# Fewer, larger tiles in four buffers, with split first loads and split last stores, in a blockwise max-pool-and-subtract kernel

## The chip, the cores and the metric

The kernel runs on one core of a Trainium2 chip. The metric is the device time of one execution in microseconds (us). The kernel before took 628.7 us, the median of four runs that lie between 628.33 and 629.75 us. A profile of one execution goes with it: the busy time of each engine, the traffic of the core's 16 DMA engines, and each instruction with its start, its duration and what it waited for.

## The reference

```python
B, C, H, W = 8, 64, 256, 256          # x: float32
x_r = x.reshape(B, C, 32, 8, 32, 8)
pooled = x_r.max(axis=(3, 5))         # max of every 8x8 block
upsampled = np.repeat(np.repeat(pooled, 8, axis=2), 8, axis=3)
return (x - upsampled).astype(np.float32)
```

Every 8x8 block of every image has its own maximum subtracted. The input and the output are 134.22 MB each.

## The kernel before, in words

The input is seen as 16,384 rows of 2,048 floats (8 KB). One such row is eight lines of an image, so it holds 32 whole blocks. A **strip** is 128 of these rows, one in each partition of on-chip memory: 1 MB. There are 128 strips in all. A tile of R strips holds, in each partition, R rows that follow one another in main memory, so that one partition's share of a transfer is one contiguous run of R x 8 KB.

The list `TILES` (L11) gives 32 tiles of four strips each. The first is loaded in two pieces of two strips, the next 30 are whole, the last is loaded in pieces of two, one and one. In this kernel a piece is the unit for loading, computing and storing alike. `BUFS = 6` (L12) gives six buffers of 32 KB per partition for the tiles, 192 KB together.

For each tile the loop at L64 takes a buffer, issues all its loads on the queue of SyncE (SP, L77), and then, piece by piece, calls `pool_and_subtract` (L36) and issues the store on the queue of ScalarE (ACT, L80). All arithmetic is on VectorE (DVE): one max-reduction for the piece (L48 for more than one strip, L41 for one strip) and then one in-place subtraction for each strip (L55). The subtraction's result overwrites the loaded data, and the store goes out of the same buffer.

The order is that of the program on each engine (L62 fixes it). Semaphores order the engines among themselves: a reduction waits for its load to land, a store waits for the last subtraction of its piece, and a load into a buffer that was used before waits until the store out of that buffer has landed. SP does nothing but issue loads, so a waiting load holds up later loads only; ACT does nothing but issue stores, so a waiting store holds up later stores only. The DMAs of both queues share the same few completion semaphores by turns, and an issue also waits until the DMA that used its semaphore earlier has landed.

Of the kernel before, what the change touches and what calls it, by code (L numbers as in the profile page):

```python
# [1 line left out]

# [4 lines left out]

F32 = mybir.dt.float32
ROW = 2048

TILES = [[2, 2]] + [[4]] * 30 + [[2, 1, 1]]  # L11
BUFS = 6  # L12


@with_exitstack
def kernel(
    ctx: ExitStack,
    tc: tile.TileContext,
    x: bass.AP,
    out: bass.AP,  # L20
):
    nc = tc.nc
    P = nc.NUM_PARTITIONS
    B, C, H, W = x.shape
    pH = pW = 8
    oW = W // pW

    x_rows = x.rearrange("b c (oh ph) w -> (b c oh) (ph w)", ph=pH)
    out_rows = out.rearrange("b c (oh ph) w -> (b c oh) (ph w)", ph=pH)
    assert sum(map(sum, TILES)) * P == x_rows.shape[0]  # L30
    size = max(map(sum, TILES))

    data = ctx.enter_context(tc.tile_pool(name="data", bufs=BUFS))
    small = ctx.enter_context(tc.tile_pool(name="small", bufs=BUFS))

    def pool_and_subtract(dat, tops, R):  # L36

        wins = dat.rearrange("p (r ph ow pw) -> p r ph ow pw", r=R, ph=pH, ow=oW)
        tops = tops.rearrange("p (r ow) -> p r ow", r=R)
        if R == 1:  # L40
            nc.vector.tensor_reduce(  # L41
                out=tops[:, 0],
                in_=wins[:, 0].rearrange("p ph ow pw -> p ow ph pw"),
                axis=mybir.AxisListType.XY,
                op=mybir.AluOpType.max,
            )
        else:
            nc.vector.tensor_reduce(  # L48
                out=tops,
                in_=wins.rearrange("p r ph ow pw -> p r ow ph pw"),  # L50
                axis=mybir.AxisListType.XY,
                op=mybir.AluOpType.max,
            )
        for r in range(R):
            nc.vector.tensor_tensor(  # L55
                out=wins[:, r],
                in0=wins[:, r],
                in1=tops[:, r].unsqueeze(1).unsqueeze(3).to_broadcast([P, pH, oW, pW]),
                op=mybir.AluOpType.subtract,
            )  # L60

    ctx.enter_context(tc.manual_schedule())  # L62
    at = 0
    for pieces in TILES:  # L64
        dat = data.tile([P, size * ROW], F32, name="dat")
        pooled = small.tile([P, size * oW], F32, name="pooled")
        parts = []
        done = 0
        for R in pieces:
            src = x_rows[at : at + P * R].rearrange("(p r) d -> p (r d)", r=R)  # L70
            dst = out_rows[at : at + P * R].rearrange("(p r) d -> p (r d)", r=R)
            part = dat[:, done * ROW : (done + R) * ROW]
            tops = pooled[:, done * oW : (done + R) * oW]
            parts.append((part, tops, dst, R))
            at += P * R
            done += R
            nc.sync.dma_start(out=part, in_=src)  # L77
        for part, tops, dst, R in parts:
            pool_and_subtract(part, tops, R)
            nc.scalar.dma_start(out=dst, in_=part)  # L80


# [1 line left out]
_INS = ['x']  # L84
_OUTS = [((8, 64, 256, 256), 'float32')]


# [23 lines left out]
```

## Time and profile before

| what | value |
|---|---|
| median of the runs | 628.7 us (628.33 to 629.75) |
| the profiled execution's own time | 628.33 us |
| its span, first to last instruction | 626.1 us |
| VectorE busy | 562.4 us, 90% |
| bytes moved | 268.46 MB, mean 429 GB/s |
| load of 4 strips, issue to landing (median) | 61.0 us |
| store of 4 strips, issue to landing (median) | 37.3 us |
| packets of 8, 16 and 32 KB, time of one on its DMA engine (packet records of the trace) | 309, 611 and 1213 ns |
| first load issued, first packet starts | 0.73 us, 1.72 us |
| last store issued, its last packet's end | 616.57 us, 624.81 us |

The span is shorter than the device time by 2.2 us, which lie before the first and after the last instruction. "GB/s" counts loads and stores together. The DMA share is the busy time of the 16 DMA engines over the stretch; it can come out a few per cent over 1.00, because records of packets overlap slightly and a packet is counted where it starts. A DMA of 128 partitions is cut into 128 packets, one for each partition, eight on each of the 16 engines; each packet is one contiguous run. A DMA's landing is the last of the 16 small writes to its semaphore, one from each engine.

### The profile page before, as it was taken

What the parts mean: (1) busy time and instruction counts of PE and PEld (TensorE: products, weight loads), DVE (VectorE), ACT (ScalarE), POOL (GpSimd) and SP (SyncE); (2) the same over time, 40 slices, a digit from 0 to 9 for tenths busy, and PEclk for the clock granted to TensorE, in tenths of its full rate; (3) what the DMA queues carried; (4) which work ended last, traced back from release to release, by engine and by line L of the source; (5) the groups of instructions that cost most, each with busy time, mean ns of one, the idle gap of its engine ahead of it and who ended that gap; (6) DMA issues with size and microseconds to landing.
All of it is one profiled execution on the core that took longest, in us unless ns stands there. A gap on an engine that the chain in (4) does not pass through costs nothing.

```text
span 626.1 us, 367 instructions
## 1 busy us (share of the span) xinstructions
DVE 562.4 (90%) x163; POOL 0.2 (0%) x4
## 2 busy tenths in 40 slices
DVE  4999999998898888988889988899888898899962
POOL 0000000000000000000000000000000000000000
DMA  9999999999999999999999999999999999999997
GB/s 366 426 421 436 425 435 435 435 435 433 435 433 434 435 435 433 431 429 431 425 435 435 435 433 433 435 433 435 435 435 433 435 427 427 431 431 432 430 442 340
DMA packets 10083, 268.46 MB, mean 429 GB/s; under 512 B 1120, under 2 KB 1120, under 8 KB 1120
## 3 DMA queue, kind: packets, MB, share of 16 engines
q1 hardware_dynamic: 5040, 134.22, 49.9%
q10 hardware_dynamic: 5040, 134.22, 49.7%
q14 instruction: 3, 0.02, 0.0%
HBM read 134.22 MB, written 134.22 MB: 429 GB/s over the span
## 4 chain that ended last, share of the span: by engine, by line
DVE 89%; another core or an unknown queue 7%; DMA 1%; issue 1%
DVE dat L55 45%; DVE pooled L48 44%; DMA dat<-in_x_dram 1%; DVE pooled L41 1%
## 5 line engine op out<-in xcount | busy, mean ns | idle before, releaser
L48 DVE TENSOR_REDUCE pooled<-dat 128x128 f32<-128x8192 f32 (+1 forms) x33 | 273.8, 8296 | 46.4 <-DMA dat<-in_x_dram 46.4
L55 DVE TENSOR_TENSOR dat<-dat,pooled 128x2048 f32<-128x2048 f32 x128 | 285.0, 2287 | 1.2
L41 DVE TENSOR_REDUCE pooled<-dat 128x32 f32<-128x2048 f32 x2 | 4.6, 2284 | 6.5 <-DMA dat<-in_x_dram 6.5
L95 POOL MEMSET const-bfloat16-1.0<- 128x1 bf16 x1 | 0.1, 101 | 0.0
L95 POOL MEMSET const-uint8-127<- 128x1 uint8 x1 | 0.1, 101 | 0.0
L95 POOL MEMSET const-float32-0.0<- 128x1 f32 x1 | 0.1, 98 | 0.2 <-issue 0.2
L95 POOL MEMSET const-float32-1.0<- 128x1 f32 x1 | 0.1, 98 | 0.0
## 6 DMA issues: line engine op xcount, KB each, us to landing
dat<-in_x_dram SPq DMA_DIRECT2D x30, 4096.0 KB, 61.0
out_dram<-dat ACTq DMA_DIRECT2D x30, 4096.0 KB, 37.3
dat<-in_x_dram SPq DMA_DIRECT2D x3, 2048.0 KB, 12.5
out_dram<-dat ACTq DMA_DIRECT2D x3, 2048.0 KB, 19.6
dat<-in_x_dram SPq DMA_DIRECT2D x2, 1024.0 KB, 66.3
out_dram<-dat ACTq DMA_DIRECT2D x2, 1024.0 KB, 13.0
```

Of the source, the lines that this page charges most:

```text
L41: nc.vector.tensor_reduce(out=tops[:, 0], in_=wins[:, 0].rearrange("p ph ow pw -> p ow ph pw"), axis=mybir.AxisListType.XY, op=mybir.AluOp ...
L48: nc.vector.tensor_reduce(out=tops, in_=wins.rearrange("p r ph ow pw -> p r ow ph pw"), axis=mybir.AxisListType.XY, op=mybir.AluOpType.max,)
L55: nc.vector.tensor_tensor(out=wins[:, r], in0=wins[:, r], in1=tops[:, r].unsqueeze(1).unsqueeze(3).to_broadcast([P, pH, oW, pW]), op=mybir ...
L95: nc = _bacc.Bacc("TRN2", target_bir_lowering=False, num_devices=1)
```

## The change

Loads and stores get lists of their own. A tile is now given by the pieces in which it is loaded and the pieces in which it is computed and stored.

- There are 22 tiles: one of four strips (loaded and stored as 1, 1, 2), one of six (3, 3 and 3, 3), 18 of six that are loaded and stored whole, one of six that is loaded whole and stored as 3, 3, and a last one of four that is loaded whole and stored as 2, 1, 1.
- There are four buffers of 48 KB per partition (192 KB as before).
- A piece is now a slice of columns of its tile. A partition's rows of the whole tile follow one another in main memory, so a piece of R strips is a run of R x 8 KB, and the runs of neighbouring partitions lie one whole tile row apart.

```diff
-TILES = [[2, 2]] + [[4]] * 30 + [[2, 1, 1]]
-BUFS = 6
+TILES = [([1, 1, 2], [1, 1, 2]), ([3, 3], [3, 3])] + [([6], [6])] * 18 + [
+    ([6], [3, 3]),
+    ([4], [2, 1, 1]),
+]
+BUFS = 4
...
-    for pieces in TILES:
+    for loads, stores in TILES:
         dat = data.tile([P, size * ROW], F32, name="dat")
         pooled = small.tile([P, size * oW], F32, name="pooled")
-        parts = []
-        done = 0
-        for R in pieces:
-            src = x_rows[at : at + P * R].rearrange("(p r) d -> p (r d)", r=R)
-            dst = out_rows[at : at + P * R].rearrange("(p r) d -> p (r d)", r=R)
-            part = dat[:, done * ROW : (done + R) * ROW]
-            tops = pooled[:, done * oW : (done + R) * oW]
-            parts.append((part, tops, dst, R))
-            at += P * R
-            done += R
-            nc.sync.dma_start(out=part, in_=src)
-        for part, tops, dst, R in parts:
-            pool_and_subtract(part, tops, R)
-            nc.scalar.dma_start(out=dst, in_=part)
+
+        rows = sum(loads)
+        src = x_rows[at : at + P * rows].rearrange("(p r) d -> p (r d)", r=rows)
+        dst = out_rows[at : at + P * rows].rearrange("(p r) d -> p (r d)", r=rows)
+        at += P * rows
+        lo = 0
+        for R in loads:
+            part = slice(lo * ROW, (lo + R) * ROW)
+            nc.sync.dma_start(out=dat[:, part], in_=src[:, part])
+            lo += R
+        lo = 0
+        for R in stores:
+            part = slice(lo * ROW, (lo + R) * ROW)
+            pool_and_subtract(dat[:, part], pooled[:, lo * oW : (lo + R) * oW], R)
+            nc.scalar.dma_start(out=dst[:, part], in_=dat[:, part])
+            lo += R
```

`pool_and_subtract` is not changed.

More of the change, by code (lines that the diff above doesn't have):

```diff
@@ L29 @@
     out_rows = out.rearrange("b c (oh ph) w -> (b c oh) (ph w)", ph=pH)
-    assert sum(map(sum, TILES)) * P == x_rows.shape[0]
-    size = max(map(sum, TILES))
+    assert sum(sum(loads) for loads, _ in TILES) * P == x_rows.shape[0]
+    size = max(sum(loads) for loads, _ in TILES)
     data = ctx.enter_context(tc.tile_pool(name="data", bufs=BUFS))
```

## The prediction

> **What bounds the kernel now.** I read the page first: the engines' busy time, the slices of DMA and GB/s, the queues.
>
> ```profile
> span 626.1 us, 367 instructions
> ...
> DVE 562.4 (90%) x163; POOL 0.2 (0%) x4
> ...
> DMA  9999999999999999999999999999999999999997
> GB/s 366 426 421 436 425 435 435 435 435 433 435 433 434 435 435 433 431 429 431 425 435 435 435 433 433 435 433 435 435 435 433 435 427 427 431 431 432 430 442 340
> ...
> q1 hardware_dynamic: 5040, 134.22, 49.9%
> q10 hardware_dynamic: 5040, 134.22, 49.7%
> ```
>
> Loads (q1) and stores (q10) together fill 99.6% of the 16 DMA engines' span. VectorE is 90% busy, but the chain of waits names it for the wrong reason: it lists what VectorE did while it stood waiting on loads in turn. The waits of VectorE and of SP's queue say so:
>
> ```profile
> DVE pooled L48 <- DMA dat<-in_x_dram: 46.4, 23, 8.8
> ...
> SPq L77 <- DMA out_dram<-dat: 501.2, 27, 19.3
> ```
>
> VectorE waits for loads, loads wait for stores to free buffers, and both run on engines that are never idle. So only three things can move the end: how long the bytes take, the idle time before the first packets, and the idle time at the end. Next the stretches (columns: stretch, length, VectorE busy, POOL busy, clock, DMA share, GB/s):
>
> ```profile
> 0.00:2.00 2.00, 0.00 (x0) 0.20 (x4) 1.00 0.65 123
> 2.00:4.00 2.00, 0.00 (x0) 0.00 (x0) 1.00 0.56 180
> 140.00:520.00 380.00, 344.45 (x100) 0.00 (x0) 1.00 1.00 433
> ...
> 612.00:616.50 4.50, 4.46 (x2) 0.00 (x0) 1.00 1.00 430
> 616.50:620.00 3.50, 0.03 (x1) 0.00 (x0) 1.00 0.96 410
> 620.00:623.00 3.00, 0.00 (x0) 0.00 (x0) 1.00 1.03 434
> 623.00:626.10 3.10, 0.00 (x0) 0.00 (x0) 1.00 0.10 40
> ```
>
> The reader should see a plateau of 433 GB/s from start to 623 us. At the head about 1.8 us are idle (first packet at 1.72 us). At the tail traffic stops at 623 to 624.8 us. The plateau is the span, so the rows for VectorE matter only as cover:
>
> ```profile
> L55 DVE TENSOR_TENSOR dat<-dat,pooled 128x2048 f32<-128x2048 f32 x128 | 285.0, 2287 | 1.2
> L48 DVE TENSOR_REDUCE pooled<-dat 128x128 f32<-128x8192 f32 x30 | 260.5, 8684 | 37.7 <-DMA dat<-in_x_dram 37.7
> L48 DVE TENSOR_REDUCE pooled<-dat 128x64 f32<-128x4096 f32 x3 | 13.2, 4415 | 8.8 <-DMA dat<-in_x_dram 8.8
> L41 DVE TENSOR_REDUCE pooled<-dat 128x32 f32<-128x2048 f32 x2 | 4.6, 2284 | 6.5 <-DMA dat<-in_x_dram 6.5
> ```
>
> **Step 1, packets.** The bytes stay; the packets get fewer. By the packet records 8, 16 and 32 KB take 309, 611 and 1213 ns: 301.3 ns per 8 KB and 7.7 ns per packet. The 433 GB/s plateau gives 16 x 32,768 B / 433 GB/s = 1210.8 ns between 32 KB packets, so about 5.5 ns each show in the wall time. Packets per engine before: 240 + 24 + 16 = 280 in each queue, 560. After, loads: 152 of 48 KB, 8 of 32, 16 of 24, 8 of 16, 16 of 8 = 200; stores: 144 of 48, 32 of 24, 16 of 16, 32 of 8 = 224; together 424. The 136 fewer save 0.75 us (5.5 ns) to 1.05 us (7.7 ns). DMAs fall from 70 to 53, 17 semaphore writes of 9 ns: 0.15 us. I take **-0.9 us**. A 48 KB packet isn't in the trace. At the low end it is one packet of 1815 ns; at the high end it is cut into three of 16 KB, then there are 1,016 packets, 456 more than before: +2.5 to +3.5 us; cut into 8 KB, 1,904 packets, +7.4 us or more. Each of the three sizes seen moved as one packet per partition, so I take one packet, and keep the cut as a rival.
>
> A rule that speaks against the ramp: the Trainium skill, "DMA: Bandwidth & Descriptors", section "Bandwidth", gives a 1 MB transfer 341 GB/s, 6.15 us, and advises larger ones. The change has six 1 MB transfers, before has four; by that figure two more cost an estimated 2 x (6.15 - 2.4) = 7.5 us. The stretch 620 to 623, all 1 MB stores, moved at 434 GB/s, so with the queue behind them they cost nothing here; the measurement decides.
>
> **Step 2, head.** The first load is 1 MB instead of 2, so its landing falls from 8.7 to about 6.3 us (2.4 us less data) and VectorE starts that much earlier. That is worth **0**: the DMA engines are the bound, and they run loads from 1.8 us either way. Four buffers hold 22 strips of loads, before 24; 22 x 2.42 us reach to 55 us with loads alone. The first buffer is free long before: VectorE ends tile 0 at 6.3 + 2 x 4.6 + 8.9 = 24.4 us, its stores land below 40 us. Seven load issues of 0.46 us each on SP lie beside 2.4 us or more of data each. Bounds -0.5 to +0.5 us.
>
> **Step 3, the middle.** A six-strip tile needs 2 x 8 x 1.813 = 29.0 us of DMA. VectorE needs 8.68 + 2 x 2.135 = 12.95 us for the reduction (2.135 is the step per strip between the rows for two and four strips) and 6 x 2.225 = 13.35 us for subtractions (8.90 us for four on the timeline), 26.4 us with the gaps. Cover is 2.6 us per tile, before 19.4 - 17.6 = 1.8. If it went, each of 19 tiles would cost its shortfall. A buffer's round is 4 x 29.0 = 116 us; less VectorE's 26.4, 89.6 us remain for a load and a store in flight. Each needs 29.0 us beside the other plus about 3.5 us (a store at 17.74 us had its first packet at 21.14), 65 together. So both queues have work and the engines don't idle: **0**. A store that waits for a semaphore that a load used last does no harm: before, VectorE ended a tile at 537.7 and its store left at 556.99, and the plateau held because loads took the share.
>
> **Step 4, the tail.** This is where something new can be late: the last tile is loaded whole, so nothing of it can start before all has landed. Count from t = 0, where tile 19 of 0 to 21 has landed in steady state. The load of tile 20 began 1.8 us earlier. It lands at 29.0. VectorE ends 19 at 26.4, waits to 29.0, then two pieces of three strips (6.55 + 6.7 = 13.25 each): stores issued at 42.3 and 55.5. The load of tile 21 (32 KB packets, 9.7 us alone) runs beside 48 KB stores. In the trace packets of the queues alternate one for one: the 16 KB load beside 32 KB stores took 14.7 us (570.9 to 585.6) for 4.9 us of work, a third. So this load gets 1213 / (1213 + 1815) = 40% and takes 24.2 us: 27 + 24.2 = 51.3, landed about 53.3. VectorE is busy to 55.5, so the whole load is hidden, by 2.2 us. Then 8.9 us for two strips and 4.6 us for each of the last: stores issued at 64.4, 69.0, 73.6.
>
> The DMA work left at t = 0: load 20 13.6, load 21 9.7, stores 18 and 19 14.0 + 14.5 (18 was issued at -2.6), store 20 14.6, store 21 9.8, together 76.2 us, plus whatever backlog b of store 17 is left. The last store needs 73.6, plus 1 us (the first load) to 3.5 us from issue to first packet, plus 2.5 us of data: 77.1 to 79.6. Idle time is then 0.9 - b to 3.4 - b. For b I have only the ramp's order: VectorE catches up with loads at tile 3, when a store has about 3.7 us beside loads left as the next is issued, 1.3 to 1.8 us of work. Before, b was near 8 us and no idle time came. Bounds 0 and 3.4; I take **+0.4 us**, nearer the lower bound, since the DMA engines are then nearly free and the first load's 1 us is the nearest row.
>
> **Step 5, the end spread.** The last store's engines ended between 623.07 and 624.81 us. After a short dry spell they would start together, worth up to -1; 48 KB packets could spread them more, up to +0.5. I take 0.
>
> Sum: -0.9 + 0.4 = -0.5, a span of 625.6 us, 627.8 with the 2.2 us around it. The profiled execution lies 0.4 us below the median, so **628.2 us**.
>
> **The rivals.**
> - *Faster.* Steps 1 and 5 at their best and no dry spell: -1.2 - 1.0 = -2.2, 626.5 us. For it: the work sum allows it, and nothing but the tail can idle. Against: all three must hold. 22%.
> - *The tail runs dry (slower).* One mechanism at one place: the stores of tile 21 follow a whole load, and VectorE's 18.1 us after it outlast the backlog. If b is 0 and the last landings are spread, 4.2 us idle, -0.9 + 4.2 = +3.3, 632.0 us. It decides when more than 2.2 us are idle (1.3 + 0.9). For it: only 2.2 us of cover over load 21, only two stores in flight. 13%.
> - *48 KB rows don't stay whole (the change doesn't do what it says).* +2.9, 631.6 us at 16 KB; 8 KB pieces 636 or more. Against: three sizes, each whole. 10%.
> - *Forecast*: 627.5 to 629.9 us, 55%.
>
> A measurement of this kernel can tell about 0.2%, 1.26 us, from no change. Faster 22%, same 55%, slower 13 + 10 = 23%. The range 626.8 to 631.0 leaves out the best of the faster case (6%), the upper dry tails (4%) and most cut rows (8%).
>
> **What would show it.** Step 1: 424 x 16 = 6,784 data packets in all, and 434 GB/s in the middle. Step 2: first packet near 1.7 us, no slice under 420 after the first. Step 3: VectorE waits of about 2.6 us per tile. Step 4: the last load landed before VectorE ends tile 20, and a short drop of GB/s before the last store. A plateau under 430, or a wait of VectorE for tile 21, would make the prediction wrong.

## The result, and the profile after

The changed kernel takes **633.07 us**, the median of 41 runs from 627.38 to 639.5 us; the kernel before 628.52 us, the median of 62 runs. The ratio is 1.005, with a 95% interval of 1.0037 to 1.0063. (This and the later intervals leave out runs over 1.5% above the fastest of their kernel, so this ratio is smaller than that of the two medians.) The kernel is slower by some 0.5%, by something no rival named, and its runs scatter over 12 us where those before scatter over less than 5.

The profiled execution took 632.22 us, with a span of 630.4 us. Its page, the lines that answer to those of before:

```profile
span 630.4 us, 319 instructions
...
DVE 560.7 (89%) x156; POOL 0.2 (0%) x4
...
DMA  9999999999999999999999999999999999999995
GB/s 374 409 440 432 437 429 451 405 449 446 409 440 446 418 433 443 430 424 446 437 412 449 443 418 433 446 427 424 449 433 415 449 446 402 449 433 423 429 431 222
...
q1 hardware_dynamic: 3600, 134.22, 49.5%
q10 hardware_dynamic: 4032, 134.22, 49.3%
```

VectorE does the same work. The DMA engines are full in every slice but the last, which moved 222 GB/s where before it was 340. The 7,632 packets of the two queues less 53 x 16 = 848 semaphore writes are the 6,784 data packets that step 1 counted. So the loss sits in the last slice. The stretches around it (stretch, length, VectorE, POOL, clock, DMA share, GB/s):

```profile
140.00:520.00 380.00, 340.71 (x92) 0.00 (x0) 1.00 1.00 434
618.00:620.00 2.00, 0.00 (x0) 0.00 (x0) 1.00 1.01 430
620.00:622.00 2.00, 0.00 (x0) 0.00 (x0) 1.00 1.02 430
622.00:624.00 2.00, 0.00 (x0) 0.00 (x0) 1.00 0.35 147
624.00:626.00 2.00, 0.00 (x0) 0.00 (x0) 1.00 0.06 25
626.00:628.00 2.00, 0.00 (x0) 0.00 (x0) 1.00 0.07 29
628.00:630.40 2.40, 0.00 (x0) 0.00 (x0) 1.00 0.02 10
```

And the kernel before:

```profile
620.00:622.00 2.00, 0.00 (x0) 0.00 (x0) 1.00 1.01 426
622.00:624.00 2.00, 0.00 (x0) 0.00 (x0) 1.00 0.65 274
624.00:626.10 2.10, 0.00 (x0) 0.00 (x0) 1.00 0.03 12
```

The plateau is 434 GB/s up to 622 us, as forecast. Then the DMA share is 0.06 for five microseconds. **One engine of sixteen is 1/16 = 0.0625.** Fifteen engines are done at 622.5 to 623.6 us, and one works on alone to 629.09 us.

How it got there can be read from the landings. Each DMA writes to its semaphore once from each engine. (Unless said otherwise, times of landings in this text are the ends of these writes in the packet records; the updates of the semaphore come 0.3 to 0.4 us later.) From the first of these 16 writes to the last but one, and to the last, for some loads of the changed kernel (us):

```
first engine lands at   128.0  186.0  244.0  331.1  389.1  476.2  563.4
last but one, later by   0.58   0.60   0.84   0.89   0.89   1.69   1.77
last, later by           0.90   1.69   3.02   3.67   5.03   5.27   5.62
```

One engine falls behind, load by load, while the rest stay within 1.8 us of one another. In the loads of the kernel before the last engine is 2.0 to 2.1 us behind from 53 to 539 us and no more. The packet records name no engine, but an engine's packets follow one another within 3 to 4 ns, so its chain can be followed back from the last packet (477 records, the full number of one engine). After 106 us its packets take 6.0 us more in all than their usual times. 3.7 us of that are in nine packets that are the first of a load (0.64, 0.55, 0.84 and 0.78 us are the longest); the engine is never idle. I call this **drift**: an engine that is out of step with the others has more of the slow packets and falls further back. No wait of an instruction shows it, since all engines always have work; it is paid at the end.

### The profile page after: what moved, and what is told of

It is laid out like the page before. It is cut to its first block, busy times and chain, and to the rows that moved or that the text cites. A ratio compares the mean times of both kernels' runs of the same rounds, so it can differ in the third digit from the quotient of the medians.

```text
span 630.4 us, 319 instructions
## 1 busy us (share of the span) xinstructions
DVE 560.7 (89%) x156; POOL 0.2 (0%) x4
## 4 chain that ended last, share of the span: by engine, by line
another core or an unknown queue 60%; DMA 21%; DVE 15%; SPq 1%; issue 0%
DMA dat<-in_x_dram 14%; DVE dat L58 7%; DMA out_dram<-dat 7%; DVE pooled L51 7%; SPq L78 1%; DVE pooled L44 1%
## 5 line engine op out<-in xcount | busy, mean ns | idle before, releaser
L51 DVE TENSOR_REDUCE pooled<-dat 128x192 f32<-128x12288 f32 (+2 forms) x24 | 268.1, 11172 | 46.7 <-DMA dat<-in_x_dram 46.7
L44 DVE TENSOR_REDUCE pooled<-dat 128x32 f32<-128x2048 f32 x4 | 9.1, 2280 | 5.4 <-DMA dat<-in_x_dram 5.4
## 6 DMA issues: line engine op xcount, KB each, us to landing
dat<-in_x_dram SPq DMA_DIRECT2D x19, 6144.0 KB, 36.7
```

The source lines that it names most:

```text
L44: nc.vector.tensor_reduce(out=tops[:, 0], in_=wins[:, 0].rearrange("p ph ow pw -> p ow ph pw"), axis=mybir.AxisListType.XY, op=mybir.AluOp ...
L51: nc.vector.tensor_reduce(out=tops, in_=wins.rearrange("p r ph ow pw -> p r ow ph pw"), axis=mybir.AxisListType.XY, op=mybir.AluOpType.max,)
```

## The experiments

The first explanation was theory A: the ramp. The landing times of the changed kernel's stores of tile 0 and 1 are late (the last piece of tile 1 was issued at 49.8 us and landed at 95.6), because stores in small packets get a small share beside loads in 48 KB packets. The load queue ran dry: one load had landed at 94.6 us, the next was issued at 96.1 and had its first packet at 100.7. B blamed the 48 KB packets, C the four buffers. All edits are to `TILES` and `BUFS` unless a diff says more; each run's ratio is to the kernel before, run beside it.

**Run 1, the head's stores whole.**

```diff
-TILES = [([1, 1, 2], [1, 1, 2]), ([3, 3], [3, 3])] + ...
+TILES = [([1, 1, 2], [4]), ([3, 3], [6])] + ...
```

> The changed kernel with the first two tiles stored whole (4 and 6 strips) instead of in pieces; their loads stay split. Theory A, late loads: the ramp's small store packets get a small share beside 48 KB load packets, so the first buffers come free late, the load queue runs dry near 94 us, and from then on each load is issued only about 3 us before the one ahead of it ends; its first packet on some engine is slow each time, and this piles up on one DMA engine that ends alone. Then here the fifth and sixth loads are issued by about 48 and 80 us, loads take about 50 us from issue to landing instead of 36.7, no engine ends alone, the runs lie close together near 627.5 us. Theory B, large packets: 48 KB packets make the slow packets themselves; then the time stays near 632 with a spread of some 10 us, and one engine ends alone. Theory C, four buffers: like B.

630.76 us, ratio 1.0035 (1.0022 to 1.0048). The queue never ran dry, the loads were 46 us in flight, and yet the landings of a load came to lie 8.6 us apart. Theory A falls as the only cause: a dry queue isn't needed.

**Run 2, no ramp with 48 KB.**

```diff
-TILES = [([1, 1, 2], [1, 1, 2]), ([3, 3], [3, 3])] + ...
+TILES = [([4], [4]), ([6], [6])] + ...
```

> The changed kernel with the first two tiles loaded and stored whole: no ramp at all. Theory A: as in the first run, loads in flight for about 50 us, about 627.5 to 628.5 us (VectorE starts some 6 us later, which costs nothing), little spread. Theories B and C: near 632 us with a spread of some 10 us.

627.81 us, 0.9992 (0.9983 to 1.0); landings up to 4.9 us apart. Large packets and four buffers alone don't cost anything, against B and C. The tail is that of the changed kernel too, so of the change's parts it is the split head that brings the loss (633.07 with it; run 1, with its loads alone split, lies between).

**Runs 3 and 4, 32 KB tiles with the ramp's first tile, in four and in six buffers.**

```diff
-TILES = ... BUFS = 4
+TILES = [([1, 1, 2], [1, 1, 2])] + [([4], [4])] * 30 + [([4], [2, 1, 1])]
+BUFS = 4        # run 4: BUFS = 6
```

> Tiles of four strips (32 KB) as in the kernel before, but in four buffers; the first tile loaded and stored in pieces of 1, 1, 2, the last loaded whole and stored as 2, 1, 1. Theory A: a round of a buffer is 4 x 19.4 = 77.4 us, less 17.6 for VectorE, 59.8 for load and store, of which each needs 19.4 and some 3.5; if loads come out near 25 us from issue to landing, they are issued late and the spread appears, if 35 us, not. Theory B: close to the kernel before, 628.5 to 629.5, little spread, whatever the queues do. Theory C: slow and scattered, 631 to 640.

> The kernel before with its six buffers of 32 KB, but with the ramp's first tile (loaded and stored as 1, 1, 2) and the last tile loaded whole. Theories A, B and C alike: loads are in flight for about 60 us, 628.0 to 629.5 us, little spread. If it is slow or scattered, the pieces at the ends are to blame and all three are wrong.

Four buffers: 629.02 us (1.0 to 1.0017), landings at most 2.9 us apart from 140 us on. Six: **676.74 us**, 1.0773 (1.0735 to 1.0812). All three theories had that run as safe. The page of the run with six:

```profile
span 674.2 us, 368 instructions
...
DMA  9999999999999999999999999999999999794684
GB/s 382 429 418 437 420 422 424 422 432 416 424 424 411 432 416 430 422 416 428 412 422 430 420 428 426 422 412 414 418 399 418 381 406 400 297 424 191 272 354 179
...
dat<-in_x_dram SPq DMA_DIRECT2D x31, 4096.0 KB, 63.0
```

The busy digits are 9 to slice 34, but the rate behind them is 420 GB/s and falls: packets take longer. In the landing records two engines are 10 us behind at 138 us and 17 and 20 us at 265 us, and near the end (digits 7, 4, 6) the other engines idle while they wait. Long queues are no protection. (That four buffers stay in step is not shown to be due to the buffers: the stores of run 3 also end at another moment, as the table below shows.)

**Runs 5 to 8: what starts it, and how far it goes.** Run 5 is the kernel before with one line changed, run 6 its opposite (pieces of 2, 2, but as column slices, and the last tile whole), run 7 has no pieces at the head, run 8 is run 4 in five buffers.

```diff
-TILES = [[2, 2]] + [[4]] * 30 + [[2, 1, 1]]
+TILES = [[1, 1, 2]] + [[4]] * 30 + [[2, 1, 1]]                               # run 5
+TILES = [([2, 2], [2, 2])] + [([4], [4])] * 30 + [([4], [2, 1, 1])]          # run 6, BUFS = 6
+TILES = [([4], [4])] * 31 + [([4], [2, 1, 1])]                               # run 7, BUFS = 6
```

> The kernel before with one edit: its first tile in pieces of 1, 1, 2 strips (each still its own contiguous rows) instead of 2, 2. The first four runs leave this theory D: the 16 DMA engines get out of step when stores in small packets start beside loads in larger ones, an engine out of step has slow packets and falls further behind, and six buffers leave it room to. Then this kernel drifts: 650 to 680 us, the landings of one DMA on its 16 engines 10 us or more apart. Rival F: the column slices, 8 KB rows 32 KB apart, are the trigger; then this kernel is like the one before, 628 to 629.5 us, landings 2 to 3 us apart.

> Six buffers of 32 KB as before, first tile in pieces of 2, 2, but as column slices of one tile, and the last tile loaded whole and stored as 2, 1, 1. Theory D (the small pieces 1, 1, 2 start it): 628 to 629.5 us, landings 2 to 3 us apart. Rival F (the column slices start it): 650 to 680 us.

> Six buffers of 32 KB, every tile loaded whole and all but the last stored whole: all packets 32 KB until the last tile. Theory D: nothing gets the engines out of step, landings 1 to 2 us apart, 627.5 to 628.5 us. If engines drift without any small packet, 635 us or more, and D is wrong in what starts it.

> The ramp 1, 1, 2 and whole last tile with 32 KB tiles in five buffers, between the runs with four (629.0 us, landings at most 3 us apart) and six (676.7 us, up to 40 us apart). Theory D with the room that the queues leave as the bound of the lag: one tile more in flight than with four, so the lag can reach some 10 to 20 us: 635 to 660 us. If the lag is not bounded by the room, this is either like four (629) or like six (677).

Run 5: 654.78 us (1.0244 to 1.0386), landings 12 us apart; here the 16 engines fan out, none is alone. Run 6: 628.43 us (0.9979 to 1.0007). So neither the column slices nor the whole last tile do harm. Run 8: 678.91 us, like six buffers, though one of its four runs took 644.52. How far the last engine is behind the first in run 4 and in run 8, for some loads (us, from the semaphore's updates):

```
run 4, first engine lands at  128.1  245.4  342.3  452.6  557.8
last, later by                 10.4   19.9   27.1   44.9   47.6
run 8, first engine lands at  128.3  246.5  352.5  458.2  563.8
last, later by                 11.5   24.0   24.4   24.3   24.1
```

With five buffers the lag comes to rest at 24 us, with six at some 45: one buffer more is room for one tile more. But the room sets the lag, not the loss. The last engine's loads land every 21.1 us in run 4 and every 21.3 us in run 8, every 19.4 us in the kernel before, and the kernel ends when the slowest engine has done its share.

Run 7 went against me: no small packet anywhere in the head, and 632.42 us (1.0033 to 1.0074; one of its four runs took 643.56) with landings 7.2 us apart. So D is wrong in what starts the drift; small packets are not needed.

**Runs 9 to 12: the moment of the first store.** Sorting the runs by when a store ends against when a load ends (on the engines that lead) gave theory G. On each engine load and store packets alternate (in the late engine's chain above the queue changes at 204 of 234 steps from one packet to the next, between 130 and 560 us), so a stagger that arises when stores join the loads stays. The four edits add no DMA and move none but in time:

```diff
+    first = True
...
+            for _ in range(EXTRA if first else 0):
+                nc.vector.tensor_reduce(    # strip 0 into pooled[:, 0:oW], overwritten afterwards
...
+            first = False
```

> The kernel before with one more one-strip max-reduction (2.28 us, its result is overwritten) ahead of the first one, so that the first store starts 2.28 us later; no DMA is changed. Theory G, the stagger: what decides is at which of a load's eight packets (per engine) the first store begins, because from then on load and store packets alternate and the stagger stays. In the runs so far the store's end came 2.5 and 4.8 us ahead of a load's end (one and two packet pairs) or half a DMA away in the runs that stayed in step, and 2.5 and 4.8 us after it in those that drifted. 2.28 us are nearly two load packets (1.21 us each) and move the stagger from one pair ahead to about one behind: this kernel drifts, 640 to 680 us, landings of one DMA 10 us apart or more. Rival H: the pieces and packet sizes of the head decide, not the stagger: then nothing changes, 628 to 629.5 us.

> The kernel with six buffers of 32 KB and no ramp (632.4 us, landings up to 7.8 us apart, store's end 4.8 us after the load's), with two more one-strip reductions ahead of the first: the first store starts 4.57 us later, nearly four load packets. Theory G: stagger goes from two pairs behind to about two ahead (six of eight), the engines stay in step, landings at most 3 us apart, 628 to 629 us. Rival H: 631.5 to 636 us as without them.

> 48 KB tiles in four buffers, no ramp (627.8 us, 626.5 to 629.2, landings up to 4.9 us apart, store's end 12.6 us from the load's, some four and a half packet pairs of 3.6 us), with two more one-strip reductions ahead of the first: first store 4.57 us later, two and a half load packets of 1.8 us. Theory G: stagger near one pair ahead, landings at most 3 us apart, 626.5 to 627.5 us with little spread, faster than both kernels. Rival H: unchanged, 627.8 with a spread of 2.7 us.

> The kernel before with its first tile in pieces of 1, 1, 2 (654.8 us, 644.6 to 664.2, landings up to 22 us apart, store's end 2.5 us after the load's), with three more one-strip reductions ahead of the first: first store 6.85 us later, more than five load packets. Theory G: stagger from one pair behind to about one or two ahead, engines in step, 628 to 629.5 us, so a ramp of small pieces does no harm by itself. Rival H: 645 to 665 us as without them.

All four moved the way G says. The kernel before, disturbed by 2.28 us of VectorE time at its start, takes 632.38 us, 1.0047 (1.003 to 1.0064). It drifts, if less than expected (5.5 us, not 10). (Undisturbed, it took 632.75 us in one of the 31 executions beside runs 13 to 16.) The two drifting kernels are cured: run 10 takes 627.58 us, 0.9982 (0.9973 to 0.9991); run 12 takes 628.17 us, 0.999 (0.9981 to 0.9999), where the same DMAs without the delay took 654.78. Run 11 takes **626.73 us, 0.9969 (0.9958 to 0.9981)**, the fastest of all, with runs from 626.55 to 627.88. The ends of run 9 and of run 11 (columns as above):

```profile
620.00:624.00 4.00, 3.02 (x2) 0.00 (x0) 1.00 0.97 414
624.00:628.00 4.00, 0.00 (x0) 0.00 (x0) 1.00 0.71 299
628.00:631.50 3.50, 0.00 (x0) 0.00 (x0) 1.00 0.09 40
```

```profile
140.00:520.00 380.00, 354.49 (x94) 0.00 (x0) 1.00 1.00 434
...
620.00:622.00 2.00, 0.00 (x0) 0.00 (x0) 1.00 1.03 434
622.00:624.00 2.00, 0.00 (x0) 0.00 (x0) 1.00 0.28 119
624.00:625.00 1.00, 0.00 (x0) 0.00 (x0) 1.00 0.00 0
```

Run 11 has the same plateau as the changed kernel, and no engine works alone after 624 us. All kernels with 32 KB tiles side by side (stagger: end of a store less the end of the nearest load, to within some 0.7 us, since it differs by engine; spread: widest landings of one DMA, load or store, between 140 and 560 us, for runs 4 and 8 by the semaphore's updates):

| kernel | buffers | stagger, us | spread, us | median, us |
|---|---|---|---|---|
| before | 6 | -2.5 | 2.2 | 628.5 |
| run 6 | 6 | -4.8 | 2.5 | 628.43 |
| run 10 | 6 | -7.2 | 2.2 | 627.58 |
| run 12 | 6 | -3.5 | 2.1 | 628.17 |
| run 3 | 4 | 9.7 either way | 2.9 | 629.02 |
| run 9 | 6 | +2 to 0 | 5.5 | 632.38 |
| run 7 | 6 | +4.8 | 7.2 | 632.42 |
| run 5 | 6 | +2.5 | 12.6 | 654.78 |
| run 4 | 6 | +2.5 at first | 47.7 | 676.74 |
| run 8 | 5 | +2.5 at first | 32.4 | 678.91 |

Stores that end before the load, or half a DMA away, go with engines in step; stores that end up to two packet pairs (4.8 us) after it go with drift. Runs 5 and 12, 7 and 10, and before and 9 differ in nothing but the added reductions, which move the start of the stores, so there the moment is shown to be the cause.

**Runs 13 to 16: the changed kernel itself.** The same delay on the changed kernel (one, two, three extra reductions) and on run 1 (two).

> The changed kernel with one more one-strip max-reduction (2.28 us, result overwritten) ahead of the first, so that its first store starts 2.28 us later; no DMA is changed. Theory G (the moment at which the stores join the loads decides whether the engines drift): at least one of this run and the next two stays in step, its landings at most 4 us apart and its runs within 1.5 us of one another near 627 us. Theory A2 (the load queue running dry near 95 us sets one engine behind, and it drifts from there): all three scatter over 5 us or more, medians 630 to 635 us.

> The changed kernel with two more one-strip reductions ahead of the first (4.57 us). Expectations of both theories as for one: G, at least one of the three in step near 627 us with a spread under 1.5 us; A2, all three scattered, 630 to 635 us.

> The changed kernel with three more one-strip reductions ahead of the first (6.85 us). G: at least one of the three in step near 627 us with a spread under 1.5 us; A2: all three scattered, 630 to 635 us, this one most, since the first buffers come free latest.

> The changed kernel with the first two tiles stored whole (630.8 us, landings up to 8.6 us apart, store's end 14.5 us from the load's, load queue never dry), with two more one-strip reductions ahead of the first. Theory G: the stagger moves by about two and a half packet pairs, landings at most 4 us apart, 626.5 to 627.5 us. If the stagger isn't what decides in 48 KB tiles, 629 to 632 us as without them.

631.1 us (628.04 to 633.64), 631.13 (629.04 to 631.68), 631.99 (628.4 to 634.77) and 630.37 (627.53 to 632.68); ratios 1.0029, 1.0034, 1.0043 and, for run 16, 1.0019 (0.9998 to 1.004). Here G fails: none is cured. In all three variants of the changed kernel, as in the kernel itself, the load queue runs dry between 90 and 98 us and the stagger then comes out at 7.3 to 9.3 us ahead, whatever the first store does. With 48 KB tiles such a stagger isn't safe: in the profiled execution of run 13 the engines stayed within 2.4 us (span 626.0), in that of run 14 they drifted to 5.8 us (629.5). Nearly the same stagger, about -7, is in run 11, whose runs scatter little and whose queue was not dry. A2 fits these four, though run 14 scatters over 2.6 us, not the 5 expected; but runs 1 and 16 drift without a dry queue, so it isn't the only way in. Their stores end 14.5 us from a load, half a DMA, which went with engines in step in run 3. So what starts the drift in the changed kernel stays open.

**Runs 17 and 18: addresses.** Run 4 with whole tiles in groups of three and of two, so that neighbouring partitions read runs 96 or 64 KB apart instead of 32.

```diff
-        src = x_rows[at : at + P * rows].rearrange("(p r) d -> p (r d)", r=rows)
+        src = x_rows[span].rearrange("(p t r) d -> t p (r d)", t=GROUP, r=rows)[pick]
```

> The kernel with six buffers of 32 KB and the ramp 1, 1, 2 (676.7 us), with the 30 whole tiles taken in groups of three: a tile takes every third block of four rows, so that the 32 KB runs of neighbouring partitions lie 96 KB apart instead of 32. Packets, DMAs, order and result are the same. Theory I (engines out of step collide over main-memory addresses): the drift changes, below 655 us or above 690. Rival J (addresses have no part): 670 to 682 us, landings 20 us or more apart.

> The same with groups of two: the 32 KB runs of neighbouring partitions lie 64 KB apart, a power of two again. Theory I: the drift changes, most likely less than with 96 KB if powers of two are what is bad: 660 to 700 us. Rival J: 670 to 682 us as without it.

671.45 us (ratio 1.0635 to 1.0741) and 674.94 us (1.0673 to 1.075), landings up to 45.6 and 48.0 us apart, 47.7 in run 4. The distance between the rows has little or no part in it. Why a packet of an engine out of step is slow **stays open**.

## Why the prediction was wrong

- *Step 1 (packets, -0.9 us): right.* The 48 KB packet moves whole, in 1815 ns, and the plateau is 434 GB/s. Run 11 against run 10, both in step, is 626.73 against 627.58: -0.85 us, which holds the packets and the small differences of their heads and tails. The page that the step names (the Trainium skill, "DMA: Bandwidth & Descriptors", section "Bandwidth") advises DMAs of at least 1 MiB. A piece of one strip is 1 MiB, so that rule did not speak against the ramp.
- *Step 2 (head, 0): right in the sum, wrong in the stores.* VectorE started at 5.4 us (6.3 forecast). But tile 0's last store landed at 55.7 us, not below 40, and the load of tile 5 was issued at 96.1. I had the rule that packets alternate and small ones get a small share, and used it at the tail only. DMA engines didn't idle for it, but loads came to be issued late, 36.7 us in flight. Several slices lie under 420 GB/s (402 to 418), which the step ruled out; so they do in run 13's execution in step (413 to 418), and the mean from 140 to 520 us is 434. The loads and stores in flight:

```profile
dat<-in_x_dram SPq DMA_DIRECT2D x19, 6144.0 KB, 36.7
out_dram<-dat ACTq DMA_DIRECT2D x18, 6144.0 KB, 53.7
```

- *Step 3 (middle, 0): right as a mean, wrong as a model.* The waits of VectorE for loads come to 2.9 us each (46.7 us in 16), 2.6 forecast:

```profile
DVE pooled L51 <- DMA dat<-in_x_dram: 46.7, 16, 3.6
DVE pooled L44 <- DMA dat<-in_x_dram: 5.4, 1, 5.4
```

  No engine idles. But I took 16 engines that are always busy for engines that all move the same; one was busy with slower packets, 6.0 us more in all.
- *Step 4 (tail, +0.4 us): the mechanism was right, the term was 0.* The last load landed at 593.9 us, 1.9 us before VectorE came to it (2.2 forecast):

```profile
589.21 6.70 DVE L58 TENSOR_TENSOR dat<-dat,pooled 128x2048 f32<-128x2048 f32 x3
595.83 4.41 DVE L51 TENSOR_REDUCE pooled<-dat 128x64 f32<-128x4096 f32 x1
```

  The last store was issued at 613.84 us, and traffic stayed at 430 GB/s to 622: no dry spell. The rival of the dry tail is refuted, and so is that of cut rows.
- *Step 5 (end spread, 0, at most +0.5 us): this is the step that failed.* The last store's engines ended between 622.47 and 629.08 us, 6.6 us apart, where before it was 1.7. The step took the spread to be a matter of the last store alone, and it had grown since 106 us, on one engine with 6.0 us of slower packets. Without the late engine the span would be some 624.9 us: 623.6 for the last of the fifteen and 1.3 us from there to the end, as before. 625.6 was forecast. The fastest runs, 627.38 and 627.63 us, are close to the 627.8 us of the sum.

So the sum held for the work, and what was missing was a term of its own: drift of single engines. It is worth nothing to some 12 us in the changed kernel and up to 50 us in its neighbours. The trace of before had the one hint: landings 2 us apart that stay apart. It couldn't show what another start would do.

## What to carry to other kernels

A DMA engine that is always busy isn't always fast: when a kernel is bound by transfers, read the landings of single DMAs engine by engine, and read a DMA share of 1/16 in the last microseconds as one late engine. A small change at the start (a split first store, two microseconds of extra work) can decide whether engines stay in step for the whole run, so an edit of a head or a tail is to be judged by several runs and its spread, and a delay of the first store is a cheap thing to try (it cured runs 5 and 7, and not the changed kernel). Where packets of two queues alternate one for one, a store in small packets beside a load in large ones gets only its share by size, and the buffer it frees is late (here 7.3 us of 24 KB packets, beside 48 KB loads, took 20 us).

## What the runs showed of the hardware that was not expected

- Engines out of step have slower packets, up to 1.2 us more for one of 32 KB that usually takes 1.21 us (run 4), and the lag grows to some 24 us with five buffers and 45 with six, while with four buffers and the same ramp it stays under 4 us (2.9 from 140 us on).
- Between 100 and 560 us the 32 KB packets of all engines together took 0.9 us more than their usual time in the kernel before, 0.9 and 2.0 in runs 10 and 12, but 13, 55, 154, 214 and 347 in runs 7, 9, 5, 4 and 8. With 48 KB this sum doesn't tell the two apart: 9.8 us in the changed kernel, 9.4 in run 13's execution in step. What differs there is that 5.7 of the 9.8 fell on one engine.
- 2.28 us of added VectorE work at the start cost 3.9 us at the end (run 9), and 6.85 us of it gained 26.6 us in another kernel (run 12 against run 5), with no DMA changed.
- The distance of rows in main memory (32, 64 or 96 KB) made little difference: 676.74, 674.94 and 671.45 us.
- Rows of 48 KB moved as single packets of 1815 ns, six times the 301 ns per 8 KB and 8 ns.
